# Two transformer blocks on one core: where the bias and post-norm tiles are loaded, and in which pieces the first activations come

## The chip, the cores and the metric

The kernel runs on one core of a Trainium2 chip. The metric is device time in microseconds (us) for one execution of the whole program, read as the median of several runs.

## The reference

Two blocks follow each other on one sequence of 256 tokens of width 1024, all in float32.

```python
x = first_block(x, mem, ...)          # rms norm, pooling mixer + attention, cross attention on mem, conv FFN
m = silu(c) @ w_mod + b_mod           # six rows of 1024: shift, scale, gate, twice
mc = silu(c_ctx) @ w_mod + b_mod
hx = modulate(x, norm_attn_pre, sh1, sc1); hc = modulate(ctx, norm_attn_pre, csh1, csc1)
mix_x = concat(latent_attention(hx, hc), fourier_mix(hx)) @ w_out
x = x + g1 * rms_norm(mix_x, norm_attn_post)
hx2 = modulate(x, norm_ffn_pre, sh2, sc2)
y = moe(hx2)                          # 32 experts, 4 per token, three matrices of 1024 x 1024 each
return x + g2 * rms_norm(y, norm_ffn_post)
```

The bias is `b_mod`; the post-norm rows are `norm_attn_post` and `norm_ffn_post`, which are multiplied by the gates g1 and g2.

## The kernel before, in words

All weights ahead of the experts lie in one packed array and come in chunks of 128 partitions x 2048 floats (1 MB) through a ring of four buffers (`RING_A`). Each chunk `w` but those of `w_mod` is split into two reduced-precision parts: ScalarE writes the high part `wh` (L325), VectorE the rest `wl` (L326), in pieces of 1024 columns, into two buffers each (`HL`). Activations are split in the same way into `ah` (L328) and `al` (L329). A product then takes three matmuls: high by high, low by high, high by low (L439 to L441, or L432 to L434). x is kept with its 1024 features on the partitions, as `xT`, eight pieces of 256 tokens.

`prog` holds the work as a list of steps with the chunks that each one needs; `emit` (L397) walks it. Before a step it issues the loads of chunks up to four ahead (`load_chunk`, L372) and the conversions of the next ones (`convert_chunk`, L384). All these loads, and small ones that ride beside certain chunks (`beside`, L362), go out through the queue of SyncE (SP) by `load` (L352). Five kinds of load go through the software queue of GpSimd (POOL) instead: the bias `brow` (L703) and the post-norm tiles `gate` (L707) of the modulation, the memory `memT`, the context `ctxT` and some constants `conM`; and, for the experts, `bdn`.

The order written in the code is not the order on an engine: the scheduler of the language puts what is ready and free ahead of what waits. Within one queue the order is then fixed, and an instruction that waits holds up those behind it.

The first step splits xT (`start`, L556), the first matmuls are those of the first chunk of `w_in` (L439), which needs features 0 to 3 of xT in two column pieces of the chunk; chunk 0 is loaded in two halves (L377). `xT` itself comes in two halves: features 0 to 3 ahead of chunk 0, 4 to 7 behind it.

The modulation is computed in three passes r = 0, 1, 2 of eight steps k (`mod_step`, L696), one chunk of `w_mod` each, which are spread as filler between the steps of the first block. In step 0 of a pass the bias is loaded into `brow`, a tile with a single buffer, and, for r of 1 and 2, one post-norm row is loaded into every partition of `gate0` or `gate1`. In step 7 VectorE adds `brow` to the sums (L715). `mod_cols` (L718) multiplies the gates into the post-norm tiles (L732) after the pass.

In the experts' part, 384 chunks of 1 MB come through 20 buffers by `load_to` (L1491) on the same queue of SyncE; the first buffers become free while the second block's attention ends.

Of the kernel before, what the change touches and what calls it, by code (L numbers as in the profile page):

```python
# [14 lines left out]
AF = mybir.ActivationFunctionType  # L15
# [6 lines left out]
P = 128  # L22
T = 256
D = 1024
# [230 lines left out]
def network(ctx: ExitStack, tc: tile.TileContext, A):  # L255
    nc = tc.nc
# [3 lines left out]
    keep = ctx.enter_context(tc.tile_pool(name="keep", bufs=1, side="left"))  # L260
    small = ctx.enter_context(tc.tile_pool(name="small", bufs=2, side="left"))
# [3 lines left out]
    def new(pool, shape, dt=F32, *, name, tag=None, bufs=None):  # L265
        kw = {}
        if bufs is not None:
            kw["bufs"] = bufs
        return pool.tile(shape, dt, name=name, tag=tag or name, **kw)

    pools = {}
# [25 lines left out]
    xT = new(ringx, [P, KD, T], name="xT", tag="w")  # L297
# [38 lines left out]
    def bank(tag):  # L336
        return new(pools["psum"], [P, 512], name="ps_" + tag, tag=tag, bufs={"a": 4, "m": 2, "f": 1, "g": 1}[tag])

    prog = Program()
    S = {}  # L340
# [11 lines left out]
    def load(t, a):  # L352
        return lambda: nc.sync.dma_start(t, a)

    def late_loads():
        load(wrt, A["w_router"])()
        load(bexp, A["b_exp"])()
        load(wf, A["wf"])()

    load(vec, A["vec"])()  # L360
    load(xT[:, :4], A["xT"][:, :4])()
    beside = {0: [load(xT[:, 4:], A["xT"][:, 4:])],  # L362
              1: [load(con["con"], A["con"]),
                  load(qkb, bass.AP(tensor=A["qkb"].tensor, offset=A["qkb"].offset, ap=[[0, P], [1, 128 + NE]]))],
# [7 lines left out]
    def load_chunk(i):  # L372
        key = order[i]
        n = CHUNKS[key[0]]
        w = new(ring[0], [P, 2048], name="w")
        src = A["wall"][CHUNK_AT[key[0]]:CHUNK_AT[key[0]] + P * n].rearrange("(p n) -> p n", p=P)
        half = n // 2 if i == 0 else n  # L377
        for o in range(0, n, half):
            nc.sync.dma_start(w[:, o:o + half], src[:, o:o + half])
        for fn in beside.get(i, ()):  # L380
            fn()
        W[key] = [w, None, None]
# [14 lines left out]
    def emit():  # L397
# [16 lines left out]
        for fn, w in prog.items:  # L414
            after = None
            if w:
                at = where[w[-1]]
            while nl < (len(order) if "out2" in marks else min(len(order), at + RING_A)) and prog.late.get(order[nl][0]) in marks:
                load_chunk(nl)
                nl += 1  # L420
            if isinstance(fn, str):
                marks.add(fn)
            else:
                convert_to(at + 1)
                after = fn(*[W.pop(k) for k in w])
            convert_to(at + 1 + HL)
            if callable(after):
                after()
# [40 lines left out]
    def tmp512(tag, bufs):  # L469
        return new(pools["tail"], [P, 512], name=tag, bufs=bufs)  # L470
# [225 lines left out]
    def mod_step(r, k):  # L696
        def fn(w):
            if r == 0 and k == 0:
                nc.scalar.activation(cT, cT, AF.Silu)
            if k == 0:  # L700
                S["mod"] = bank("g")
                S["brow"] = tmp512("brow", 1)
                nc.gpsimd.dma_start(S["brow"], A["bmod"][r])  # L703
                if r:
                    i = r - 1
                    S["gate", i] = new(keep if i else pools["tail"], [P, D], name="gate%d" % i, bufs=1)
                    nc.gpsimd.dma_start(S["gate", i], bass.AP(tensor=A["post"].tensor, offset=A["post"].offset + i * D,  # L707
                                                              ap=[[0, P], [1, D]]))
            ps = S["mod"]
            for g in range(4):  # L710
                nc.tensor.matmul(ps[32 * g:32 * g + 32, :], cT[:, k, :], w[0][:, 512 * g:512 * g + 512],
                                 start=k == 0, stop=k == 7)
            if k == 7:
                m = S["mrow", r] = tmp512("mrow", 1)
                nc.vector.tensor_tensor(m, ps, S.pop("brow"), op=ALU.add)  # L715
        return fn
# [959 lines left out]
    for n, e in enumerate(experts):  # L1676
# [38 lines left out]
        for h in range(2):  # L1715
            r = slice(64 * h, 64 * h + 64)
# [72 lines left out]
```

## Time and profile before

| what | value |
|---|---|
| median of 3 runs | 1551.59 us (1550.2 to 1551.77) |
| profiled execution, its own time | 1554.47 us |
| its span in the profile | 1552.5 us |
| TensorE counted busy | 1465.9 us (94%) |
| VectorE, ScalarE, GpSimd busy | 603.9, 431.3, 5.1 us |
| SyncE's hardware queue (q1) | 507.80 MB |
| GpSimd's software queue (q0) | 4.78 MB |
| mean of all queues | 332 GB/s |

The span runs from the first to the last instruction that the profile shows; the execution's own time has 2 us more. Busy shares are means over stages that differ: up to some 600 us three-matmul products with many conversions beside them, after that matmuls of the experts beside a stream of their weights. So a question on one stage is put to the views of that stage. In the views, a bracket behind an instruction tells how long its engine sat idle before it and what ended that; "issue" to "landing" of a transfer includes the time that it stands in its queue behind others.

### The profile page before, as it was taken

The numbers are of one execution on the slowest core, as the hardware profiler recorded it, in microseconds if no ns is written. First come the engines' busy times: TensorE is split into PE (matmuls) and PEld (weight loads), VectorE is DVE, ScalarE is ACT, GpSimd is POOL, SyncE is SP. The second block draws the span as 40 slices with busy tenths as digits, with TensorE's granted clock in tenths as the row PEclk, the third lists the DMA queues.
The fourth block names the chain that finished last, engine by engine and source line by source line (L and its number), as shares of the span: only waits on it lengthen the run. The fifth ranks groups of instructions, "written<-read, shape, count | busy, mean of one in ns | idle before, by whom it ended". The sixth has DMA issues, their size and how long they took to land. (4 is left out here: it accounts for less than half of the span.)

```text
span 1552.5 us, 20127 instructions
## 1 busy us (share of the span) xinstructions
PE 1465.9 (94%) x7985; PEld 831.0 (54%) x7985; DVE 603.9 (39%) x1436; ACT 431.3 (28%) x781; POOL 5.1 (0%) x13
## 2 busy tenths in 40 slices
PE   7999999999999998999999999999899999999996
PEld 5787888789998765333433333333334333333332
DVE  7859668666767465122212112112121122121113
ACT  5545655544547542111101111101111011011111
POOL 0000000000000000000000000000000000000000
PEclk9989999999999998999999999999999999999999
DMA  9645465886532448999999999999999999999993
GB/s 345 234 159 173 153 222 194 316 300 230 190 123 94 163 170 334 388 425 425 426 424 427 424 426 426 424 425 426 408 415 425 425 426 424 426 425 426 424 426 148
DMA packets 72883, 514.82 MB, mean 332 GB/s; under 512 B 8112, under 2 KB 8880, under 8 KB 11920
## 3 DMA queue, kind: packets, MB, share of 16 engines
q1 hardware_dynamic: 71712, 507.80, 80.8%
q0 software_dynamic: 1008, 4.78, 0.8%
q8 instruction: 110, 1.80, 0.4%
q14 instruction: 53, 0.43, 0.1%
HBM read 511.50 MB, written 1.05 MB: 330 GB/s over the span
## 5 line engine op out<-in xcount | busy, mean ns | idle before, releaser
L1615 PE MATMUL p_g<-w,xs 128*64 128x512 f32 x2112 | 461.1, 594 | 0.7 <-issue 0.7
L1615 PEld LDWEIGHTS p_g<-w,xs 128*64 128x64 f32 x2112 | 148.7, 137 | 310.8 <-issue 295.8
L1647 PE MATMUL p_t<-w,aT 128*64 128x512 f32 x1056 | 235.4, 598 | 2.2 <-ACT aT L1635 2.2
L326 DVE TENSOR_TENSOR wl<-w,wh 128x1024 fp32r<-128x1024 f32 (+3 forms) x150 | 173.1, 1178 | 50.2 <-ACT wh L325 50.0
L325 ACT ACTIVATE wh<-w 128x1024 fp32r<-128x1024 f32 (+3 forms) x150 | 146.8, 1016 | 132.9 <-issue 39.0
L1621 DVE TENSOR_SCALAR hg<-p_g 128x512 f32<-128x512 f32 x33 | 22.8, 692 | 378.9 <-PE p_g L1615 378.9
L1647 PEld LDWEIGHTS p_t<-w,aT 128*64 128x64 f32 x1056 | 73.2, 137 | 149.3 <-issue 130.1
L439 PE MATMUL ps_a<-wh,ah 128*128 128x512 f32 (+3 forms) x240 | 92.1, 387 | 12.7 <-ACT wh L325 11.1
L432 PE MATMUL ps_m<-ah,wh 128*128 128x256 f32 x352 | 101.6, 289 | 1.4 <-ACT wh L325 1.4
L1623 ACT ACTIVATE hs<-hg 128x512 f32<-128x512 f32 x33 | 20.8, 629 | 289.9 <-DVE hg L1621 289.9
L434 PE MATMUL ps_m<-ah,wl 128*128 128x256 f32 x352 | 100.4, 285 | 0.0
L433 PE MATMUL ps_m<-al,wh 128*128 128x256 f32 x352 | 100.4, 285 | 0.0
L1720 ACT ACTIVATE z<-p_t 64x512 f32<-64x512 f32 x63 | 37.3, 592 | 207.5 <-PE p_t L1647 207.1
L441 PE MATMUL ps_a<-wl,ah 128*128 128x512 f32 (+3 forms) x240 | 92.3, 385 | 0.0
L440 PE MATMUL ps_a<-wh,al 128*128 128x512 f32 (+3 forms) x240 | 91.8, 383 | 0.0
L1626 DVE TENSOR_SCALAR hu<-p_g 128x512 f32<-128x512 f32 x33 | 22.8, 692 | 154.7 <-PE p_g L1615 154.7
L1656 PE MATMUL p_y<-z,gt 128*128 128x512 f32 x128 | 63.9, 605 | 18.8 <-ACTq L1680 18.1
L1558 PE MATMUL p_t<-sel,x 128*128 128x128 f32 (+1 forms) x544 | 70.7, 285 | 11.2 <-ACT aT L1635 11.2
L1558 PEld LDWEIGHTS p_t<-sel,x 128*128 128x128 f32 x544 | 64.7, 195 | 28.6 <-issue 14.6
L1566 ACT ACTIVATE xs<-p_t,modT,A 128x128 f32<-128x128 f32 (+1 forms) x68 | 30.8, 453 | 158.9 <-PE p_t L1558 146.7
L432 PEld LDWEIGHTS ps_m<-ah,wh 128*128 128x128 f32 x352 | 68.1, 194 | 9.3 <-issue 3.4
L434 PEld LDWEIGHTS ps_m<-ah,wl 128*128 128x128 f32 x352 | 68.1, 194 | 2.4 <-DVE wl L326 0.8
(368 smaller groups left out, 1787.1 us busy)
## 6 DMA issues: line engine op xcount, KB each, us to landing
w<-w_gate_dram SPq DMA_DIRECT2D x128, 1024.0 KB, 19.6
w<-w_up_dram SPq DMA_DIRECT2D x128, 1024.0 KB, 19.5
w<-w_down_dram SPq DMA_DIRECT2D x127, 1024.0 KB, 19.6
w<-wall_dram SPq DMA_DIRECT2D x89, 1024.0 KB, 4.9
w<-wall_dram SPq DMA_DIRECT2D x4, 768.0 KB, 4.1
w<-wall_dram SPq DMA_DIRECT2D x3, 576.0 KB, 3.8
w<-wall_dram SPq DMA_DIRECT2D x2, 640.0 KB, 3.9
xT<-xT_dram SPq DMA_DIRECT2D x2, 512.0 KB, 7.7
```

The source lines that it names most:

```text
L325: nc.scalar.activation(hi, src, AF.Copy)
L326: nc.vector.tensor_tensor(lo, src, hi.bitcast(F32), op=ALU.subtract)
L432: nc.tensor.matmul(o, sh, mh, start=start, stop=False, **kw)
L433: nc.tensor.matmul(o, sh, ml, start=False, stop=False, **kw)
L434: nc.tensor.matmul(o, sl, mh, start=False, stop=stop, **kw)
L439: nc.tensor.matmul(o, a, wh, start=start, stop=False)
L440: nc.tensor.matmul(o, b, wh, start=False, stop=False)
L441: return nc.tensor.matmul(o, a, wl, start=False, stop=stop)
L1558: nc.tensor.matmul(ps[:, i * n * SLOTS:(i + 1) * n * SLOTS], x4[:, t, j * P:(j + 1) * P], sel[:, t].rearrange("p a b -> p (a b)"), start=t ...
L1615: last = nc.tensor.matmul(ps[64 * h:64 * h + 64, :], xs[:, 2 * c + jj, i * SLOTS:(i + 1) * SLOTS], w[:, jj, 512 * h:512 * h + 512], start= ...
L1647: nc.tensor.matmul(po[64 * h:64 * h + 64, :], s, w[:, jj, o:o + 512], start=c == 0 and jj == 0, stop=c == 3 and jj == 1)
L1656: nc.tensor.matmul(yb[t][h], gt[:, h, t * P:(t + 1) * P], z[:, h], start=False, stop=stop, skip_group_check=True)
```

## The change

The first xT transfer brings features 0 and 1 only; features 2 and 3 are loaded between the two halves of chunk 0. A column of zeros is written by GpSimd and passed through ScalarE ahead of everything else, so that ScalarE's table is loaded on it. The bias and the post-norm tiles are loaded by `load`, through the queue of SyncE, the tiles at step 3 of their pass and the bias at step 5, in place of step 0 on GpSimd's queue.

```diff
+    first = new(small, [P, 1], name="first", bufs=1)
+    nc.gpsimd.memset(first, 0.0)
+    nc.scalar.activation(first, first, AF.Identity)
     load(vec, A["vec"])()
-    load(xT[:, :4], A["xT"][:, :4])()
+    load(xT[:, :2], A["xT"][:, :2])()
     beside = {0: [load(xT[:, 4:], A["xT"][:, 4:])],
...
         for o in range(0, n, half):
             nc.sync.dma_start(w[:, o:o + half], src[:, o:o + half])
+            if i == 0 and o == 0:
+                load(xT[:, 2:4], A["xT"][:, 2:4])()
         for fn in beside.get(i, ()):
             fn()
...
             if k == 0:
                 S["mod"] = bank("g")
+            if k == 3 and r:
+                i = r - 1
+                S["gate", i] = new(keep if i else pools["tail"], [P, D], name="gate%d" % i, bufs=1)
+                load(S["gate", i], bass.AP(tensor=A["post"].tensor, offset=A["post"].offset + i * D, ap=[[0, P], [1, D]]))()
+            if k == 5:
                 S["brow"] = tmp512("brow", 1)
-                nc.gpsimd.dma_start(S["brow"], A["bmod"][r])
-                if r:
-                    i = r - 1
-                    S["gate", i] = new(keep if i else pools["tail"], [P, D], name="gate%d" % i, bufs=1)
-                    nc.gpsimd.dma_start(S["gate", i], bass.AP(tensor=A["post"].tensor, offset=A["post"].offset + i * D,
-                                                              ap=[[0, P], [1, D]]))
+                load(S["brow"], A["bmod"][r])()
```

## Rows read from the trace of the kernel before

**Rows 1.** The page's head.

```profile
span 1552.5 us, 20127 instructions
```

**Rows 2.** Timeline, first 20 us: start, duration, engine, line, operation, count, idle before.

```profile
0.74 0.39 SPq L353 DMA_DIRECT2D vec<-vec_dram  x1
1.18 0.42 SPq L353 DMA_DIRECT2D xT<-xT_dram  x1
...
1.65 0.90 SPq L379 DMA_DIRECT2D w<-wall_dram  x2
1.91 1.06 POOL L707 DMA_DIRECT2D gate<-post_dram  x2
...
5.46 1.28 ACT L328 ACT_TABLE_LOAD   x1 [5.46 <-DMA xT<-xT_dram]
6.76 0.51 ACT L328 ACTIVATE ah<-xT,vec 128x256 fp32r<-128x256 f32 x1
...
9.02 1.06 ACT L325 ACTIVATE wh<-w 128x1024 fp32r<-128x1024 f32 x1 [1.76 <-DMA w<-wall_dram]
...
10.13 0.79 PE L439 MATMUL ps_a<-wh,ah 128*128 128x512 f32 x1 [10.13 <-ACT wh L325]
...
18.92 0.39 PE L439 MATMUL ps_a<-wh,ah 128*128 128x512 f32 x1
```

**Rows 3.** DMA, first 16 us; issues: count, KB each, median us to landing.

```profile
DMA packets 1451, 4.96 MB, mean 310 GB/s; under 512 B 163, under 2 KB 476, under 8 KB 1308
...
q0 software_dynamic: 368, 1.31, 22.7%
...
vec<-vec_dram SPq DMA_DIRECT2D x1, 118.5 KB, 2.1
...
xT<-xT_dram SPq DMA_DIRECT2D x1, 512.0 KB, 4.2
...
w<-wall_dram SPq DMA_DIRECT2D x1, 512.0 KB, 7.3
```

**Rows 4.** POOL's timeline; brow's and gate's readers (duration ns, first to last start).

```profile
308.10 0.54 POOL L703 DMA_DIRECT2D brow<-bmod_dram  x1 [73.97 <-DVE mrow L715]
...
L715 DVE TENSOR_TENSOR mrow<-ps_g,brow x3: 687/689/692, 232.6 to 357.6; 128x512 f32<-128x512 f32 x3
...
L732 DVE TENSOR_TENSOR gate<-gate,ps_f x4: 682/685/689, 312.6 to 369.1; 128x512 f32<-128x512 f32 x4
```

**Rows 5.** Waits of TensorE, 0 to 650 us: total us, times, longest.

```profile
PE ps_a L439 <- ACT wh L325: 11.1, 2, 10.1
PE ps_m L690 <- ACT pooled L681: 2.4, 1, 2.4
```

**Rows 6.** Windows: us; PE, PEld, DVE, ACT, POOL busy; clock, DMA share, GB/s.

```profile
40.00:60.00 20.00, 20.00 (x102) 15.02 (x101) 17.07 (x51) 8.56 (x12) 0.00 (x0) 1.00 0.69 237
600.00:650.00 50.00, 45.01 (x198) 18.93 (x200) 12.16 (x43) 7.85 (x15) 0.00 (x0) 0.83 0.93 372
...
1400.00:1500.00 100.00, 95.37 (x474) 36.70 (x474) 18.30 (x43) 12.47 (x23) 0.00 (x0) 1.00 1.01 425
```

**Rows 7.** Waits of the SyncE queue, 800 to 900 us.

```profile
SPq L1504 <- DMA w<-w_down_dram: 32.3, 15, 3.0
```

**Rows 8.** Timeline, 50 to 60 us: SyncE's issues, a conversion.

```profile
50.56 0.42 SPq L353 DMA_DIRECT2D wrt<-w_router_dram  x1
...
54.10 0.33 SPq L379 DMA_DIRECT2D w<-wall_dram  x1
...
59.00 2.00 ACT L325 ACTIVATE wh<-w 128x1024 fp32r<-128x1024 f32 x2 [0.73 <-DMA w<-wall_dram]
```

**Rows 9.** Timeline, 298 to 316 us: SyncE's issues, a conversion, TensorE.

```profile
300.17 12.57 SPq L379 DMA_DIRECT2D w<-wall_dram  x5
...
307.35 1.06 ACT L325 ACTIVATE wh<-w 128x1024 fp32r<-128x1024 f32 x1 [8.28 <-DMA w<-wall_dram]
...
308.45 0.38 PE L432 MATMUL ps_m<-ah,wh 128*128 128x256 f32 x1 [1.41 <-ACT wh L325]
```

## The prediction

> **What bounds the kernel now.** The whole span is 1552.5 us [rows 1]. I read the start in order of time first [rows 2], since the change is made there. The reader is to see a chain in which TensorE has no part yet: x's first half is issued at 1.18 us, the first weight half at 1.65, ScalarE meets both as they land, and the first matmul starts at 10.13. The table load (1.28 us) runs at 5.46, once x has landed; but behind it stands one scaling and then 1.76 us of idle time, until the weight half is there at 9.02. Its 1.06 us of conversion end at 10.1. So the front waits for the weight half, and the table load is not on that path.
>
> The transfers of the first 16 us say why the half is late [rows 3]. The weights' queue lands its transfers in order: the vectors at 0.74 + 2.1 = 2.84 us, x's half at 1.18 + 4.2 = 5.4, the weight half at 1.65 + 7.3 = 8.95. The first 0.52 MB took 2.6 us, the next 0.52 MB 3.6. Beside them the software queue moves 1.31 MB: the bias (0.26 MB) and both post-norm tiles (0.52 MB each, issued from 1.91 us on [rows 2]). All queues together made 310 GB/s here, so 1.31 MB are worth 4.2 us of it. And nothing of them is read before 232.6 us (bias) and 312.6 (tiles) [rows 4].
>
> Whether a gain at the front lives to the end is read from what TensorE waited for up to 650 us [rows 5]: the first conversion, 10.1 us, then nothing over 2.5, and nowhere a transfer itself. From 40 to 60 us it is busy all the time while DMA has 0.31 of its share free [rows 6]. Then come the experts. There DMA is saturated (1.01 and 425 GB/s at 1400 to 1500), and the SyncE queue waits for transfers to land [rows 6, 7]. But this stream gets going only as the stage before it frees buffers (0.93 from 600 to 650), so a start that is d earlier moves the saturated stream by d as a whole.
>
> **The change, part by part.**
> *Order of the front.* Ahead of the weight half stand the vectors and now 0.26 MB of x in place of 0.52. From the landing of the vectors, 2.84 us, that is 0.26 + 0.52 = 0.79 MB to go. Their price without the software queue is not in the trace. The low bound is x's own half, 0.2 MB per us with the bias beside it: 3.9 us, landing at 6.8. The high bound is the saturated 425 GB/s: 1.9 us, landing at 4.7. I take the 310 GB/s of that same stretch, nearest in place: the competing queue goes, the slow first packets stay. That makes 2.5 us, and the half lands at 5.4. With the 1.1 us that lay between landing and matmul before, TensorE starts at 6.5 in place of 10.13: **3.6 us** (bounds 2.2 and 4.3).
>
> *Does the rest keep up?* The first quarter lands at 2.84 + 0.85 = 3.7, so its scalings (0.51 us each) are over before 5.4. The second quarter and the second weight half are 0.79 MB more: 7.9. TensorE needs that half at its thirteenth matmul; the 24 of a chunk took 8.8 us (10.13 to 18.92 [rows 2]), so not before 10.9. x's second half lands near 9.6, chunk 1 (1.05 MB) near 13.0, its first half is converted at 14.1, and TensorE comes to it at 6.5 + 8.8 = 15.3. That leaves 1.2 us of margin, so I count nothing as given back.
>
> *Table load.* It waits only for a memset on POOL; even if that came as late as the tiles' issue at 1.91 us, it would end near 3.2, ahead of the first quarter. Its worth: had it stayed, it would run from 3.7 to 5.0, a scaling to 5.5, and the conversion would start 0.1 us late. So 0.1 us, in the 3.6 already. The Trainium skill (ScalarE: Activation LUTs, "What ACT_TABLE_LOAD costs") puts a drain of about 1.4 us on top of such a load. The rows show none: the activation behind it starts 0.02 us after its end [rows 2]. By the page this edit would save 1.5 us of what it would cost to leave it, and my sum would stay as it is, because the load is out of the way.
>
> *Issues on SyncE.* The third issue for x takes 0.4 us, as the others do, and comes while bytes still flow: nothing. The five moved transfers (three biases, two tiles) cost the same each. SyncE has gaps of 3 us and more between weights (50.56 to 54.10 [rows 8]): nothing, unless a wait comes with them (third rival). POOL keeps loads that wait for buffers, and loses nothing.
>
> *Where the bytes go.* Tiles emitted late are pulled ahead to where a queue is free: the router's weights, emitted after the cross attention, were issued at 50.56 [rows 8]. The first bias and both tiles wait for no buffer, so I expect them in such gaps: 1.3 MB, 3.1 us at 425 GB/s. If they stood ahead of the chunk issued at 54.10, whose conversion at 59.00 waited 0.73 us for it, each tile would delay it by 1.2 us. Cost 3.1 at most, below zero nothing, since nothing is removed there; I take 0, with 0.31 of DMA free.
>
> *Sum.* 1552.5 - 3.6 = 1548.9 in the profiled execution's span, whose own time was 1554.5; the median shown, 1551.6, is 2.9 below that. From the median: 1551.6 - 3.6 = **1548.0**. A measurement of this kernel can tell 0.2% from no change, which is 3.1 us: faster means below 1548.5.
>
> **The rivals.**
> *Part is given back.* The tiles, or another order of issue, cost one or two waits for weights between 40 and 100 us, 1 to 3 us. For it: a conversion there waits for its transfer already. Against it: DMA has room, and TensorE shows no such wait. Result near 1549.8, which counts as no change.
>
> *Each transfer pays its own latency.* A chunk of 1.05 MB alone took 4.9 us from issue to conversion (54.10 to 59.00 [rows 8]), of which 2.5 are bytes at 425 GB/s, so 2.4 are latency. Paid in series, the quarter would land at 2.84 + 2.4 + 0.6 = 5.8 and the half at 9.5: no gain, 1552. Against it: in series that one queue could never reach 425 GB/s, as it does with such chunks; 1.05 MB in 4.9 us are 214. The Trainium skill (DMA: Bandwidth & Descriptors, "Anatomy of one DMA") fits about 2.0 us + bytes/436e3 to a transfer and advises pieces of at least 1 MiB, which speaks against quarters. Added in series, its fit would land the half at 8.7 and leave a gain of 0.3 us; the saturated stretch contradicts such a sum here.
>
> *The SyncE queue blocks.* The third bias must wait until VectorE has read the second; POOL sat 74 us on that wait and issued at 308.10 [rows 4]. On SyncE all that is queued behind it waits as well, and there weights are late already: a conversion at 307.35 had waited 8.28 us for its chunk, and TensorE 1.41 for the conversion [rows 9]. SyncE issued five weight loads between 300.17 and 312.7, one per 3 us. With the bias two places too early they come 6 to 7 us late, and TensorE has no cover there: 1551.6 - 3.6 + 7 = 1555.0. It turns the sign from a stall of 3.6 us on. Against it: the bias is asked for at step 5 of its pass, long after step 7 of the pass before.
>
> *More than forecast.* TensorE's clock is granted at 0.83 from 600 to 650, and DMA moves 372 in place of 425 GB/s [rows 6], some 6 us of its stream. If the earlier start shifts that pause, up to 2 us come on top: 1546.
>
> **How the numbers follow.** Forecast 0.54, part given back 0.24, no gain at the front 0.05, blocked queue 0.08, more than forecast 0.09. That the edit does not do what it says is no case: queue and order are written out in the code. The forecast's own range is 1547.3 to 1549.4, by the front's bounds; of its 0.54 I put 0.44 below 1548.5. Faster is then 0.44 + 0.09 = 0.53, slower 0.08, same the remaining 0.39. For 8 in 10 the range leaves out the blocked queue, the front without gain and half of the last case: 1546.2 to 1551.3.
>
> **What would show it.** Right: no POOL transfer in the first 16 us, the table load over by 3.2, the first weight conversion near 5.4, the first matmul near 6.5, chunk 1 near 15.3; the same 3.6 us of lead at 60, 300 and 600 us; tiles issued in SyncE's gaps. Wrong: a first conversion after 6.8 us; a lead that shrinks between 40 and 100 us (second case) or at 300 to 370, with SyncE waiting on the bias's reader (blocked queue); a lead at 650 that is not in the total.

## The result, and the profile after

| | kernel before | kernel after |
|---|---|---|
| median, 6 runs each, run side by side | 1549.75 us (1548.28 to 1551.77) | 1558.09 us (1555.74 to 1561.51) |
| profiled execution, its own time | 1554.47 us | 1557.22 us |
| its span | 1552.5 us | 1555.3 us |

The ratio of after to before is 1.0052, with a 95% interval of 1.0042 to 1.0063: the change costs 8 us, and the forecast of 1548.0 and its range (to 1551.3) lie below every run of it.

The start does what it was meant to, by half. This is the timeline of the kernel after; it answers to [rows 2].

```profile
0.74 1.28 ACT L362 ACT_TABLE_LOAD   x1 [0.74 <-PEq L1785]
...
1.19 0.42 SPq L353 DMA_DIRECT2D xT<-xT_dram  x1
1.66 0.42 SPq L382 DMA_DIRECT2D w<-wall_dram  x1
2.03 0.20 ACT L362 ACTIVATE first<-first 128x1 f32<-128x1 f32 x1
2.12 0.43 SPq L353 DMA_DIRECT2D xT<-xT_dram  x1
...
4.21 0.91 ACT L328 ACTIVATE ah<-xT,vec 128x256 fp32r<-128x256 f32 x2 [1.98 <-DMA xT<-xT_dram]
...
7.27 1.06 ACT L325 ACTIVATE wh<-w 128x1024 fp32r<-128x1024 f32 x1 [1.63 <-DMA w<-wall_dram]
...
8.38 0.80 PE L444 MATMUL ps_a<-wh,ah 128*128 128x512 f32 x1 [8.38 <-ACT wh L325]
...
17.58 0.49 PE L444 MATMUL ps_a<-wh,ah 128*128 128x512 f32 x1
```

The table load is over at 2.02, no transfer of GpSimd stands here any more, and the first matmul starts at 8.38 in place of 10.13; chunk 1 begins at 17.58 in place of 18.92. A lead of 1.3 to 1.75 us, then, and it does not get lost on the way to the experts. (The profiled execution of before took 1554.47 us, 4.7 more than the median beside it, so a lead over it is read as too large.) The matmul that opens each block of an expert (`p_g<-bexp,con`, 264 of them) gives the start and the end of that stage; the columns behind the count are shortest, median and longest ns, then the first and the last start. Before:

```profile
L1608 PE MATMUL p_g<-bexp,con x264: 589/610/1083, 605.3 to 1512.2; 64*64 64x512 f32 x132
```

After:

```profile
L1613 PE MATMUL p_g<-bexp,con x264: 589/610/1081, 596.6 to 1510.4; 64*64 64x512 f32 x132
```

The experts begin 8.7 us earlier in this profile, the last of these matmuls starts only 1.8 us earlier, and the span ends 2.8 us later. Everything is lost in the experts' part, where the DMA engines are full. The kernel after, windows (columns as in [rows 6]):

```profile
600.00:650.00 50.00, 48.85 (x219) 18.70 (x218) 7.19 (x15) 6.54 (x11) 0.00 (x0) 0.91 0.95 375
1400.00:1500.00 100.00, 93.98 (x460) 35.86 (x457) 19.43 (x45) 11.32 (x21) 0.00 (x0) 1.00 1.01 418
```

The DMA engines are as full as before (1.01), the granted clock is 1.00, its level of 2.4 GHz, and yet 418 GB/s arrive where [rows 6] has 425. The head of the DMA part for 700 to 1100 us says it with more digits. Before:

```profile
DMA packets 23316, 170.12 MB, mean 425 GB/s; under 512 B 2585, under 2 KB 2585, under 8 KB 2585
```

After:

```profile
DMA packets 22909, 167.16 MB, mean 418 GB/s; under 512 B 2539, under 2 KB 2539, under 8 KB 2539
```

That is 2.96 MB less in 400 us, with packets of the same kind. The traces hold the time of each: a packet of 8192 bytes takes 310.2 ns in the mean before and 315.8 after, 1.8% longer. Not one of the edits touches these transfers. But the new column `first` is a tile of the pool `small`, and the placement of the compiled program gives it 32 bytes of every partition, ahead of the 20 buffers of the experts' weights. They start at byte 41216 of a partition before (161 x 256), 8192 bytes apart, and at byte 41248 after. Only they and the tiles of `small` behind the column move; the tiles of all other pools lie where they lay. That was the theory to be tested, against the rivals that the moved loads, the quarters or the new order of work slow the stream.

### The profile page after: what moved, and what is told of

It reads as the page before. It is cut to its first block, busy times and chain, and to the rows that moved or that the text cites. A ratio compares the mean times of both kernels' runs of the same rounds, so it can differ in the third digit from the quotient of the medians.

```text
span 1555.3 us, 20125 instructions
## 1 busy us (share of the span) xinstructions
PE 1465.5 (94%) x7985; PEld 826.6 (53%) x7985; DVE 603.9 (39%) x1436; ACT 432.1 (28%) x782; POOL 2.5 (0%) x9
```

## The experiments

All of them compute the whole reference. The table gathers what they gave. "Offset" is the start of the weight buffers modulo 256 bytes; "moved" the MB from 700 to 1100 us; the stage is the span less the first start of `p_g<-bexp,con`, both of one profile. The two profiles of one kernel without a column, 950.2 and 947.2, show that a single stage can be off by 3 us. Each ratio compares with runs of the kernel before in its own series (medians 1549.75 to 1551.4).

| run | column | offset | ratio to before, 95% interval | moved | experts' stage, us |
|---|---|---|---|---|---|
| before | none | 0 | 1 | 170.12 | 947.2 |
| after | 32 bytes | 32 | 1.0052 (1.0042 to 1.0063) | 167.16 | 958.7 |
| b_pad32 | 32 bytes, unused | 32 | 1.0071 (1.0054 to 1.0087) | 167.18 | 956.7 |
| a_pad64 | 64 bytes | 64 | 1.0045 (1.0027 to 1.0063) | 167.74 | 955.1 |
| a_pad128 | 128 bytes | 128 | 1.0013 (1.0001 to 1.0025) | 167.96 | 957.3 |
| a_wf | in wf | 0 | 0.9975 (0.9960 to 0.9990) | 170.10 | 947.3 |
| a_wf_again | in wf | 0 | 0.9968 (0.9955 to 0.9981) | 170.12 | 947.3 |
| a_512 | in wf | 0 | 0.9984 (0.9972 to 0.9995) | 170.12 | 947.1 |
| a_nofirst | none | 0 | 1.0000 (0.9988 to 1.0013) | 170.05 | 950.2 |
| a_nofirst_again | none | 0 | 0.9997 (0.9981 to 1.0012) | 170.08 | 947.2 |
| b_queue | none | 0 | 0.9984 (0.9968 to 1.0001) | 170.08 | 947.0 |
| b_quarters | none | 0 | 1.0002 (0.9988 to 1.0017) | 170.08 | 947.7 |
| b_first1 | in wf | 0 | 1.0004 (0.9990 to 1.0018) | 170.07 | 947.6 |

### The room alone: b_pad32 and a_wf

b_pad32 is the kernel before with a column that nothing reads:

```diff
+    spare = new(small, [P, 1], name="spare", bufs=1)
+    nc.gpsimd.memset(spare, 0.0)
     load(vec, A["vec"])()
```

> The kernel before, with one unused column of 32 bytes in the pool ahead of the weight buffers, and nothing else. Address theory: the experts begin at 605 us as before, the stream makes 417 GB/s, and the time is 1549.8 + 14 to 17, 1564 to 1567 us. Traffic theory: 425 GB/s and 1549.8 us, within 1.5 of the kernel before.

a_wf is the kernel after with its column inside a tile that is there anyway and is loaded later:

```diff
-    first = new(small, [P, 1], name="first", bufs=1)
+    first = wf[:, 0, :1]
```

> The changed kernel, but the zeroed column lies in the first column of the Fourier weights' tile, which is loaded only at about 54 us, so it takes no room of its own and all 20 weight buffers start where they did before (at byte 41216 of a partition in place of 41248). Address theory (the 32 bytes that the column takes shift the weight buffers off a multiple of 64 bytes, and the stream of the experts' weights is slower into such buffers): the stream is back at 425 GB/s from 417, the experts begin at 597 us as in the changed kernel, and the time is 1541 us (1539 to 1544). Traffic theory (the new order and queue of the loads slow the stream): 417 GB/s and 1558 us, as the changed kernel.

The unused column makes the kernel before 10 to 11 us slower (median 1561.22), with its front, its queues and its transfers as they were. The move of the column into `wf` takes the loss away: the median is 1545.82, and the ratio puts it 3.9 us under the kernel before. b_pad32 came out a few us lower than written, a_wf some 5 us higher, so the size of the lead was overrated; the sign and the place are as expected. b_pad32's head of the DMA part for 700 to 1100 us, then its windows 600 to 650 and 1400 to 1500, then its experts:

```profile
DMA packets 22914, 167.18 MB, mean 418 GB/s; under 512 B 2541, under 2 KB 2541, under 8 KB 2541
```

```profile
600.00:650.00 50.00, 48.86 (x228) 19.57 (x227) 9.22 (x25) 6.93 (x12) 0.00 (x0) 0.96 0.98 394
1400.00:1500.00 100.00, 95.06 (x469) 36.37 (x466) 18.92 (x44) 11.30 (x21) 0.00 (x0) 1.00 1.01 418
```

```profile
L1610 PE MATMUL p_g<-bexp,con x264: 589/610/1083, 599.4 to 1510.9; 64*64 64x512 f32 x132
```

And a_wf's window 1400 to 1500 and its experts:

```profile
1400.00:1500.00 100.00, 95.61 (x468) 37.32 (x466) 20.37 (x46) 11.90 (x22) 0.00 (x0) 1.00 1.01 425
```

```profile
L1613 PE MATMUL p_g<-bexp,con x264: 589/610/1083, 597.7 to 1505.0; 64*64 64x512 f32 x132
```

The stream is back at 425 GB/s and the stage at 947.3 us, so the loads, the quarters and the order of work do not slow it. b_pad32 tells a second thing: it has the front of before, but its experts begin at 599.4, not 605.3. This gap opens ahead of the stage: the first reader of the bias starts at 230.1 in place of 232.6, the first product of `conM` and `mrow` at 519.5 in place of 525.3. The granted clock differs on that way, 0.91 against 0.74 from 80 to 100 us (behind the same wait of TensorE, 2.44 us) and 0.98 against 0.95 from 400 to 500. So the start of the experts varies by some 6 us between single executions, and neither 8.7 nor the 2.8 us against b_pad32 is the lead of the change. The profile of before was slower than its median by 3 to 5 us, that of b_pad32 faster by 3. As a_wf's stage is as long as before's, its total says what the lead is in the mean: 4 to 5 us.

384 chunks of 1.0486 MB are 402.7 MB: 947 us at 425 GB/s, 963 at 418, 16 us more if the whole of it ran at the lower rate. The stage got longer by 9.5 (b_pad32) and 11.5 us (after). The end of the stage has the difference. Windows of before, then of after:

```profile
1530.00:1540.00 10.00, 9.31 (x38) 3.25 (x35) 0.69 (x1) 1.09 (x2) 0.00 (x0) 1.00 0.00 0
```

```profile
1530.00:1540.00 10.00, 7.80 (x36) 2.77 (x36) 1.14 (x2) 0.68 (x2) 0.00 (x0) 1.00 0.27 111
```

In windows of 1 us the last weights come in just after 1529 us before and just after 1537 in after and b_pad32. Counted from the stage's start the stream itself thus lasts some 924, 941 and 938 us: 17 and 14 more, near the 16. But before has 23 us of work left when its stream ends, the other two 18 and 19. TensorE was behind the stream there and is now held by it; its waits for weights from 590 us on are none in before, and in after:

```profile
PE p_g L1620 <- DMA w<-w_up_dram: 6.3, 12, 0.7
PE p_g L1620 <- DMA w<-w_gate_dram: 1.1, 2, 0.6
```

So some 5 us of the slower stream are hidden by slack that before had at its end.

### Which boundary: a_pad64, a_pad128, a_512

```diff
-    first = new(small, [P, 1], name="first", bufs=1)
-    nc.gpsimd.memset(first, 0.0)
-    nc.scalar.activation(first, first, AF.Identity)
+    first = new(small, [P, 16], name="first", bufs=1)          # a_pad128: [P, 32]
+    nc.gpsimd.memset(first[:, :1], 0.0)
+    nc.scalar.activation(first[:, :1], first[:, :1], AF.Identity)
```

> The changed kernel with a column of 64 bytes, so that the weight buffers start at 41280, a multiple of 64 bytes but not of 256. Address theory, if 64 bytes are what counts: 425 GB/s, 1541 us. Address theory, if it is 256 bytes: the stream stays slow, 417 to 420 GB/s, 1554 to 1559 us. Traffic theory: 1558 us.

> The changed kernel with a column of 128 bytes: weight buffers at 41344, a multiple of 128 but not of 256. Address theory with a boundary of 256 bytes: the stream stays below 425 GB/s, 419 to 421, 1553 to 1557 us. With a boundary of 128 bytes: 425 GB/s and 1546 us.

In time, 64 bytes bring back next to nothing. 128 bytes bring back about half: 1.0013, with an interval apart from after's. The one profiled stage of a_pad128 doesn't show that, and its stream is only a little faster, so what else the 128 bytes bring stays open. The heads for 700 to 1100 us, a_pad64 first, then a_pad128:

```profile
DMA packets 22990, 167.74 MB, mean 419 GB/s; under 512 B 2549, under 2 KB 2549, under 8 KB 2549
```

```profile
DMA packets 23023, 167.96 MB, mean 420 GB/s; under 512 B 2555, under 2 KB 2555, under 8 KB 2555
```

In the mean a packet of 8192 bytes takes 314.8 and 314.4 ns. So a multiple of 64 or of 128 does not do. The buffers of the kernel before start at an odd multiple of 256; whether a multiple of 512 does still better is asked by a_512, which is a_wf with one buffer less for a small tile, so that they start at 40960 (80 x 512):

```diff
-    rank = new(small, [P, 2, NE], name="rank")
+    rank = new(small, [P, 2, NE], name="rank", bufs=1)
```

> The changed kernel with the column in the Fourier weights' tile and one small buffer less ahead of the weight buffers, which then start at 40960, a multiple of 512 bytes (and of 4096), in place of 41216, a multiple of 256 alone. Address theory with 256 bytes: 425 GB/s as at 41216, and 1544 to 1547 us. If a wider boundary counted as well, the rate is above 426 and the time under 1543.

Its head for 700 to 1100 us:

```profile
DMA packets 23315, 170.12 MB, mean 425 GB/s; under 512 B 2584, under 2 KB 2584, under 8 KB 2584
```

Nothing beyond 256, then: 425 GB/s at both multiples of it that were run, 418 to 420 at the offsets 32, 64 and 128. Its median (1547.26) is no better than a_wf's, and just above the range that was written for it.

### The change without its column: a_nofirst, twice

The kernel after, all else as it was:

```diff
-    first = new(small, [P, 1], name="first", bufs=1)
-    nc.gpsimd.memset(first, 0.0)
-    nc.scalar.activation(first, first, AF.Identity)
     load(vec, A["vec"])()
```

> The changed kernel without the zeroed column: x in quarters and the loads on the SyncE queue stay, the table is loaded when x arrives. Address theory: 425 GB/s, 1541 to 1543 us; the first matmul comes at most 0.5 us later than 8.4. Traffic theory: 417 GB/s and 1558 to 1559 us.

> The changed kernel without the column once more, beside the column alone, since its first comparison came out 5 us behind the same kernel with a column although its first matmul came at the same time. Order theory: again 1549 to 1552 us, at 425 GB/s, with a pause of TensorE of 2 us or more near 78 us. If the first comparison was a matter of chance: 1545 to 1548.

The stream is at 425 GB/s again, which the theory needs. But the time is that of before (1.0000 and 0.9997), over 8 us above what was written for the first run. The first matmul starts at 8.8 and 8.5 us, as early as in a_wf (8.8, again 8.0). So a lead of 1.5 us at the first matmul alone is not to be seen in the total. The column, as long as it takes no room, brings 4 to 5 us in the first series (a_wf against a_nofirst) and 2 in the last (a_512 against a_nofirst_again, with intervals that overlap). The table load can't be that by its own time, since the first matmul comes no later without it.

### The parts one by one: b_queue, b_quarters, b_first1

Each is the kernel before with one part. b_queue has the last hunk of the change (bias and post-norm tiles) and no other:

```diff
...
+            if k == 5:
                 S["brow"] = tmp512("brow", 1)
-                nc.gpsimd.dma_start(S["brow"], A["bmod"][r])
...
+                load(S["brow"], A["bmod"][r])()
```

> The kernel before with only the bias and the post-norm tiles moved to the SyncE queue; x still in halves, no zeroed column, weight buffers at 41216. Queue theory (the front waited for the weight half because the software queue took its share, as forecast): 1.05 MB after 2.84 us land near 6.5 and the first matmul starts at 7.6 in place of 10.13; 1548.5 us against 1551. Slow-start theory (the first microseconds of any transfers run at some 0.18 MB per us whatever the software queue does, as the runs so far show): landing at 8.5, first matmul 9.6 or later, time within 1 us of the kernel before. Blocked-queue theory: slower by 2 us or more, with TensorE waiting behind SyncE around 230 or 310 us.

b_quarters has the pieces of `xT` alone:

```diff
-    load(xT[:, :4], A["xT"][:, :4])()
+    load(xT[:, :2], A["xT"][:, :2])()
...
+            if i == 0 and o == 0:
+                load(xT[:, 2:4], A["xT"][:, 2:4])()
```

> The kernel before with only x in quarters; the bias and the tiles stay on the software queue, no zeroed column, weight buffers at 41216. Slow-start theory: the 0.26 MB less ahead of the weight half are worth 1.3 us, first matmul at 8.8, as with the whole change, and the time 1 to 3 us under the kernel before. Queue theory: most of the gain needs the software queue gone; first matmul at 9.3 or later, time within 1 us of the kernel before.

b_first1 has the column alone, in `wf`:

```diff
-    load(vec, A["vec"])()
+    nc.gpsimd.memset(wf[:, 0, :1], 0.0); nc.scalar.activation(wf[:, 0, :1], wf[:, 0, :1], AF.Identity); load(vec, A["vec"])()
```

> The kernel before with only the zeroed column and its activation (in the Fourier weights' tile, so that nothing moves); x in halves, bias and tiles on the software queue. Hidden-load theory (the table load was not on the path, as forecast): the first matmul starts at 10.1 as before, and the time is that of the kernel before, within 1.5 us. Order theory (the scheduler, with the table load out of the way, plans another order of all engines' instructions up to the experts, and the order is what pays): the pause of TensorE near 80 us shrinks from 2.4 us to under 1.5, the clock granted from 80 to 100 us rises from 0.74 to 0.95 or more, and the time is 2 to 4 us under the kernel before.

None moves the time by what the runs can tell, b_queue with an interval that just reaches 1. b_queue lands its weight half at 8.35 (1.65 + 6.7) and starts the first matmul at 9.52, near the slow start that was written and far from the 7.6 of the queue theory; its time, 2.2 us under before's median, is nearer to what the queue theory had, so it settles neither. Three timelines show the first conversion of weights; b_queue:

```profile
8.41 1.06 ACT L325 ACTIVATE wh<-w 128x1024 fp32r<-128x1024 f32 x1 [0.45 <-DMA w<-wall_dram]
```

b_quarters:

```profile
9.69 1.06 ACT L325 ACTIVATE wh<-w 128x1024 fp32r<-128x1024 f32 x1 [3.08 <-DMA w<-wall_dram]
```

b_first1:

```profile
10.19 1.06 ACT L325 ACTIVATE wh<-w 128x1024 fp32r<-128x1024 f32 x1 [1.07 <-DMA w<-wall_dram]
```

In [rows 2] it is 9.02. b_first1, whose loads are those of before, has 10.19, so a single profile of this can be off by over 1 us, and that b_quarters comes later than before is not shown. Its first matmul, at 10.80, and its time are as the queue theory had them (9.3 or later, no gain), and not as the slow start had them (8.8). The quarters and the free queue together give 6.6 to 7.7 in eight profiles, 7.27 in after; neither does alone.

What the column does shows at 75 to 82 us, where TensorE waits for the pooled values. Before:

```profile
79.94 0.70 PE L690 MATMUL ps_m<-pooled,poolw 128*128 128x256 f32 x2 [2.44 <-ACT pooled L681]
...
86.68 2.83 PE L667 MATMUL ps_a<-pt,uv 128*64 128x256 f32 x16 [0.69 <-ACT pt L652]
```

a_nofirst:

```profile
78.45 1.57 PE L692 MATMUL ps_m<-pooled,poolw 128*128 128x256 f32 x4 [2.17 <-DVE al L329]
...
83.55 1.52 PE L669 MATMUL ps_a<-pt,uv 128*64 128x256 f32 x16 [0.69 <-ACT pt L654]
```

After:

```profile
77.12 1.50 PE L695 MATMUL ps_m<-pooled,poolw 128*128 128x256 f32 x4 [1.29 <-DVE al L329]
...
81.60 1.52 PE L672 MATMUL ps_a<-pt,uv 128*64 128x256 f32 x16 [0.69 <-ACT pt L657]
```

The order of instructions on ScalarE and VectorE is fixed when the program is built, and the column changes it: in after the first of two `pooled` is written at 71.43, ahead of a group of `s<-s`; in a_nofirst both come behind that group, from 74.47 on. A pause of 2.2 to 2.4 us becomes 1.3. The granted clock of the window behind it differs too; windows from 80 to 100 us, before, a_nofirst_again and after:

```profile
80.00:100.00 20.00, 18.72 (x114) 15.60 (x115) 6.20 (x10) 7.38 (x13) 0.53 (x1) 0.74 0.29 105
```

```profile
80.00:100.00 20.00, 19.31 (x142) 17.59 (x141) 6.19 (x9) 7.71 (x12) 0.53 (x1) 0.83 0.33 111
```

```profile
80.00:100.00 20.00, 19.31 (x165) 18.48 (x164) 8.97 (x12) 8.62 (x14) 0.53 (x1) 1.00 0.40 127
```

After the short pause it is 1.00 in after (2.4 GHz all the time), and the same matmuls of the group `ps_a<-pt,uv` take 1.52 us in place of 2.83. That lead of 5.1 us over before at 82 us is in after and in the a_wf runs. But the pause does not decide the clock: b_pad32 has before's pause of 2.44 and was granted 0.91, and b_first1 has the pause of 1.29 us, was granted 0.83, and gained nothing in time. It was expected to show whether the order alone pays, and does not settle it.

The record has one more thing, the mean granted clock of every execution. Executions with the same one, 0.986, have these medians: before 1551.8 us (22 of them), the two series of a_nofirst 1548.6 (4), the two of a_wf 1545.8 (3). So at an equal clock the change without its column does lead by 3 us. (b_first1's two at 0.986 are 1548.9 and 1549.1, too few to tell.) It is granted less, 0.983 and 0.985 in the median where before has 0.986 and 0.987, and so the lead does not reach the total. Whether the order of work causes the lower clock was not tried.

### The version that beats both: a_wf_again

> The changed kernel with the zeroed column in the Fourier weights' tile (weight buffers at 41216), once more beside the two parts alone, since the kernel without a column came out 5 us behind it at the same address. If the table load ahead of x is worth little (it ends before x lands, and the first matmul came at 8.8 in both), this is 1546 to 1550 us, within 2 us of the kernel without a column; if it is worth what the first comparison shows, it is 1545 to 1546 again. Address theory: 425 GB/s again.

The second series gives 1545.77 and a ratio of 0.9968; the first was 0.9975. The change with its column in `wf` is 0.25 to 0.3% faster than the kernel before. The kernel after ran in another series; by the ratios to before it is 12 to 13 us behind.

## Why the prediction was wrong

**The sign: a term that the sum lacks.** The step that failed is the one on the table load: "It waits only for a memset on POOL", and "So 0.1 us, in the 3.6 already." It priced the column's time, which was right (the load is over at 2.02, and nothing waits for it), and not its room. The room costs 9.5 to 11.5 us in the experts' stage: b_pad32 shows it with the room and nothing else (but the one write of the column), a_wf with all else and no room. None of the four rivals was this, and the one on the far side, the blocked queue, did not occur. The sign that the prediction named, a lead at 650 that is not in the total, is what came.

**The saturated stream "as a whole".** The sentence that a start d earlier moves the stream by d holds at an equal rate: a_wf, a_wf_again and a_512 start the experts 7.6 to 10.6 us before the profile of before and need the same 947 us. It took for granted that the 425 GB/s of [rows 6] are the stream's whatever its buffers' addresses.

**The front: a size.** Forecast was a weight half that lands at 5.4; it landed at 7.25 (1.66 + 5.6), the first matmul came at 8.38 in place of 6.5, and the gain of 3.6 us was 1.75, under its low bound of 2.2. The mis-sized term is the 310 GB/s for 0.79 MB. They took 4.4 us behind the vectors' landing, 0.18 MB per us, less than the 0.2 that x's half made with the software queue beside it. The heads of the DMA part for the first 10 us show a part of it; before:

```profile
DMA packets 768, 2.43 MB, mean 243 GB/s; under 512 B 76, under 2 KB 204, under 8 KB 768
...
q1 hardware_dynamic: 537, 1.59, 57.1%
```

After:

```profile
DMA packets 876, 2.37 MB, mean 237 GB/s; under 512 B 93, under 2 KB 221, under 8 KB 854
...
q1 hardware_dynamic: 876, 2.37, 80.2%
```

The total is the same. In after the weights' queue carries 2.37 MB in place of 1.59, so it takes over what the software queue had. But the half in front did not get all of it: of the 1.30 MB that had moved by 7.25 us, 0.39 belonged to transfers issued behind the half. And the rate from 2.84 to 7.25 was 238 GB/s. "The competing queue goes" is right, "the 310 GB/s of that same stretch" is its mean over 16 us, and the first 10 have less. In the rival with a latency for each transfer, the fit of the Trainium skill (DMA: Bandwidth & Descriptors, "Anatomy of one DMA") is one for transfers issued by GpSimd, while these were issued by SyncE; the 7.25 lies between its 8.7 and the 5.4 of the forecast.

**The rest keeps up: right.** Chunk 1's first matmul came 1.3 us earlier than before (four small matmuls now run ahead of it, from 17.22, and before ran later), and TensorE's longest wait of 20 to 650 us is 2.2, for VectorE, none for a transfer. Forecast was 15.3, it is 17.58, late like the first matmul. The lead over the profile of before does not stay the same, as forecast; it is 5.1 us at 82, 7.3 at the first reader of the bias and 8.7 at the experts, and the granted clock has its part in that.

**Issues on SyncE, and where the bytes go: right.** The bias left at 47.69, 225.98 and 333.17, the tiles in the gap at 54.73, behind the chunk that they might have delayed; that chunk's conversion runs at 58.52 without a wait. SyncE's timeline of after:

```profile
47.69 0.42 SPq L353 DMA_DIRECT2D brow<-bmod_dram  x1
52.56 0.33 SPq L382 DMA_DIRECT2D w<-wall_dram  x1
...
54.73 0.91 SPq L353 DMA_DIRECT2D gate<-post_dram  x2
```

The third bias was issued 16 us before its reader at 349.0, so nothing piled up behind it.

**The total without the column's room.** a_wf's 3.9 and a_wf_again's 5.0 us are near the 3.6 of the forecast, but that is luck and not its working: the first matmul holds 1.3 to 2.1 us of it, and a_nofirst, with nearly the same first matmul, holds nothing in the end. The rest comes with the order of work at 75 to 90 us and the granted clock, which the forecast did not treat there; its last rival had the clock at 600 to 650 us. How much of it is order and how much clock stays open.

## What to carry to other kernels

A new tile, however small, moves what is placed behind it: price its room as well as its time, and before a change is read by its total, compare the start addresses of the buffers behind it and the GB/s of a saturated stretch in both kernels. Where a stream keeps the DMA engines full, try its buffers at multiples of 256 bytes, or put a small helper into a tile that is there already. And hold the time of a profiled execution against the median before a stage's start is read from it: here one slow profile of before made a lead of 4 to 5 us look like 8.7.

## What the runs showed of the hardware that was not expected

A saturated stream of 1 MB loads from the device's memory, in packets of 8 KB for the most part, moves 425 GB/s into buffers that start at a multiple of 256 bytes of a partition, and 418, 419 and 420 at offsets of 32, 64 and 128, with the DMA engines counted as full (1.01) each time. Its packets of 8192 bytes take 310.2 ns in before and 315.8, 314.8 and 314.4 at these offsets. Two profiles at offset 32 (167.16 and 167.18 MB) agree within 0.05%, and so do nine at offset 0 (170.05 to 170.12).

The Trainium skill (DMA: Bandwidth & Descriptors, "How a descriptor splits into AXI transactions") says that a transfer's piece that doesn't start on a 256-byte boundary has its first transaction begin at the boundary below, so that bytes are fetched and not used. The page words it for reads; here the shifted addresses are those written to. Of the offsets that were run, only the multiples of 256 are fast, so a boundary of 256 bytes fits. By that page's count an estimate for an 8 KB piece is 257, 258 and 260 units of 32 bytes in place of 256, a loss that grows with the offset (0.4, 0.8, 1.6%); measured is one that shrinks, 1.8, 1.4 and 1.3%. So what makes the packets longer stays open; it was not tried, nor were offsets above 128.

In the first 10 us the queues together move 2.3 to 2.5 MB in all runs, by one queue or by two (2.37 after, 2.43 before), and splitting or freeing them changes mainly whose bytes these are.

The granted clock of a stretch differs between single executions of kernels with the same front and the same wait before it (0.74 and 0.91 from 80 to 100 us in before and b_pad32). With this stretch and that from 400 to 500 us (0.95 and 0.98) go most of the 5.9 us by which their experts' starts differ.
